# Priority for attention's small VectorE operations, and a scan carry of four operations, in a two-layer hybrid decoder trunk

## The chip, the cores and the metric

The kernel runs on one core of one Trainium2 chip. The metric is the device time of one execution in microseconds (us). Before the change it is 2682.31 us, the median of three runs (2680.16 to 2685.91).

## The reference, cut to what matters

The reference is a trunk of two layers on a residual stream of 256 tokens by 2048 features, all in float32. In each layer one input projection makes queries, keys and values (8 heads), the input of a state-space branch (1024 wide) and two gates.

- Branch A is a causal differential attention. Each head has two score maps; both go through a softmax, and the second map, times a learned lambda, is subtracted from the first. The weighted values are divided by their root mean square per head (`lax.rsqrt(mean(o^2) + 1e-5)`) and scaled.
- Branch B is a diagonal complex state-space model: 64 groups of 16 channels, each driving 64 complex states, scanned causally over the 256 tokens: `h[t] = a * h[t-1] + B u[t]`, `y = Re(C h) + D u`, then GELU and a gated linear unit.

Each branch has its own up-projection; the two are gated, summed and go through an output projection. Layer norm, an MLP with squared ReLU (2048 to 8192 to 2048) and a second layer norm follow.

## The kernel before, in words

**The matmuls.** Every float32 weight and activation is split into a high part, rounded to the type float32r, and a low part, the rest. A product is three matmuls: high by high, high by low, low by high. Weights come in chunks of 512 KB through one DMA queue (line 337). For each chunk ScalarE writes the high part `whi` (line 142) and VectorE the low part `wlo` (line 144); there are three buffers of each, and one chunk is prepared ahead (`AHEAD = 1`). The matmuls of a chunk are at lines 469, 470 and 473 (`tok_mul`, tokens on the output's rows), 544 to 546 (`gemm_feat`) and 567 (`gemm_up`); the one at line 470 reads `wlo`.

**The background.** Attention (`attn_gen`) and the state-space branch (`ssm_gen`) are Python generators. After each weight chunk of the projections the program takes some of their steps (`bg.pump`), so their instructions are traced in between the chunks'. They fill VectorE and ScalarE while TensorE multiplies. `bg.finish(agen)` traces what is left of attention before the attention up-projection, which reads attention's result `ahl`, and `bg.finish(sgen)` what is left of the scan before the gated linear unit.

**The order on each engine** is fixed when the program is built. A planner (Tile's scheduler, with a timeline of its own, `schedule_with_timeline_sim=True`) gives each engine, whenever the engine is free on that timeline, the instruction with the lowest priority number among those that it takes to be ready. The number is the place in the traced order. Inside `with tc.high_priority():` an instruction counts as from the program's start, and so goes ahead of everything that is ready with it. The kernel already does this in two places: the three operations of the rotary embedding (lines 927 to 929) and the gate of the attention up-projection (line 1001).

**Attention's chain, for each pair of heads** (four pairs in a layer). For each head: scores on TensorE (line 789), maxima on VectorE (796), exponentials with their sums on ScalarE (799), the sums' reciprocals (802) and the second one times minus lambda (803) on VectorE, the second map scaled on ScalarE (805), the two maps combined on VectorE (806), transposes on TensorE (811). For the pair: the product with the values (817 to 819), squares with their sums on ScalarE (823), the mean (825) and the inverse root on VectorE: a seed (319) and three Newton steps of three operations each (325, 326, 327), every one on the result of the one before; then the scaling on ScalarE (830), transposes on TensorE (835), and the result's high part on ScalarE (838) and low part on VectorE (839).

**The scan** goes over 4 groups in a layer and in each over 4 chunks of 64 tokens, real and imaginary part apart. At each of the 3 boundaries between chunks six small operations on 128x8 elements carry the state on: two copies of the last state (749), two products with the decay `s_r` (731) and two additions to the first input of the next chunk (732). Then two scan instructions follow (735), then the turning of the chunk by complex factors (739 to 745).

Of the kernel before, what the change touches and what calls it, by code (L numbers as in the profile page):

```python
# [11 lines left out]
F32 = mybir.dt.float32  # L12
# [4 lines left out]
ALU = mybir.AluOpType  # L17
# [3 lines left out]
P = 128  # L21
# [9 lines left out]
L = 64  # L31
# [3 lines left out]
RMS_EPS = 1e-5  # L35
# [69 lines left out]
def trunk(ctx: ExitStack, tc: tile.TileContext, A, out):  # L105
    nc = tc.nc
    V, SC, GP, PE = nc.vector, nc.scalar, nc.gpsimd, nc.tensor
# [89 lines left out]
    s_r = const([P, 64], "s_r")  # L197
# [4 lines left out]
    neglam = const([P, DEPTH], "neglam")  # L202
# [118 lines left out]
    def rsqrt(o, v, n):  # L321
        rsqrt_seed(o, v)
        for _ in range(3):
            a = sm([P, n], tag="rsa", bufs=2)
            V.tensor_tensor(a, o, o, op=ALU.mult)
            V.scalar_tensor_tensor(a, a, -0.5, v, op0=ALU.mult, op1=ALU.mult)
            V.scalar_tensor_tensor(o, a, 1.5, o, op0=ALU.add, op1=ALU.mult)
# [328 lines left out]
    def ssm_gen(l, st):  # L656
        lp = l * 32
        e_re = slot([P, 4, 8, L], name="e_re")
        e_im = slot([P, 4, 8, L], name="e_im")
        w = [slot([P, NCH, 8, L], name="sw") for _ in range(2)]  # L660

        def load_c(g):
            cz = tmp.tile([P, 2, 8, 32], F32, tag="cz", name=nm("cz"), bufs=2)
            hold(GP.dma_start(cz, cmem[l][g] if l in cmem else A["cT"][l, g]))
            return cz

        for g in range(4):
            if l in emem:
                for t, e in zip((e_re, e_im), emem[l]):
                    drip.append((t[:, g], e[:, g]))  # L670
            else:
                for step in e_steps(l, g, e_im[:, g], e_re[:, g]):
                    yield 0.1 if isinstance(step, tuple) else step
        cz_next = load_c(0)
        while st["u"] is None:
            yield 0.5

        def operands(i):
            if i == 16:
                return None  # L680
            g, j = i // 4, i % 4
            bs = tmp.tile([P, 2, 2, P], F32, tag="bs", name=nm("bs"), bufs=1)
            us = tmp.tile([P, 2, 256], F32, tag="us", name=nm("us"), bufs=1)
            b = bsplit[l][g // 2][j, :, :, g % 2].rearrange("r m h c -> m r (h c)")
            u = st["split"][g // 2][j, :, :, 2 * (g % 2):2 * (g % 2) + 2].rearrange("r m h t -> (r m) (h t)")
            for m in range(2):
                ms = slice(64 * m, 64 * m + 64)
                GP.dma_start(bs[ms].rearrange("p h c s -> p (h c s)"), b[m][:, None].broadcast_to([32, 2, 512]))
                GP.dma_start(us[ms].rearrange("p h t -> p (h t)"), u)
            return bs, us  # L690

        nxt = operands(0)
        uT = st["u"]
        for g in range(4):
            jj = slice(lp + 8 * g, lp + 8 * g + 8)
            cz = cz_next
            cz_next = load_c(g + 1) if g < 3 else None
            rt = t_bg([P, 8, L])
            SC.activation(rt, s_r[:, jj, None].broadcast_to([P, 8, L]), AF.Copy)
            GP.memset(rt[:, :, 0:1], 0.0)  # L700
            yield 0.1
            if l not in cmem:
                c_steps(l, g, cz)
                yield 2.0
            for k in range(4):
                bs, us = nxt
                bu = psa.tile([P, 2, 2, NCH, L], F32, tag="bu", name=nm("bu"), bufs=1)
                for q in range(2):
                    for ri in range(2):
                        PE.matmul(bu[:, q, ri].rearrange("p a b -> p (a b)"), bs[:, q, ri, :].bitcast(F32R), us[:, q, :].bitcast(F32R), start=True, stop=True)  # L710
                nxt = operands(4 * g + k + 1)
                yield 0.3
                er = e_re[:, g, k::4, None, :].broadcast_to([P, 2, NCH, L])
                ei = e_im[:, g, k::4, None, :].broadcast_to([P, 2, NCH, L])
                wr, wi = (w[ri][:, :, k::4, :].rearrange("p c q t -> p q c t") for ri in range(2))
                ta, tb = t_bg([P, 2, NCH, L]), t_bg([P, 2, NCH, L])
                V.tensor_tensor(wr, bu[:, :, 0], er, op=ALU.mult)
                V.tensor_tensor(ta, bu[:, :, 1], ei, op=ALU.mult)
                V.tensor_tensor(wi, bu[:, :, 1], er, op=ALU.mult)
                yield 1.8  # L720
                V.tensor_tensor(tb, bu[:, :, 0], ei, op=ALU.mult)
                V.tensor_tensor(wr, wr, ta, op=ALU.add)
                V.tensor_tensor(wi, wi, tb, op=ALU.subtract)
                yield 1.8
            rg = rt.rearrange("p a b -> p (a b)")
            er, ei = e_re[:, g], e_im[:, g]
            carry = None
            for c in range(NCH):
                if c > 0:
                    for ri in range(2):  # L730
                        V.tensor_tensor(carry[:, ri, :], carry[:, ri, :], s_r[:, lp + 8 * g:lp + 8 * g + 8], op=ALU.mult)
                        V.tensor_tensor(w[ri][:, c, :, 0], w[ri][:, c, :, 0], carry[:, ri, :], op=ALU.add)
                for ri in range(2):
                    wv = w[ri][:, c].rearrange("p a b -> p (a b)")
                    V.tensor_tensor_scan(wv, rg, wv, 0.0, ALU.mult, ALU.add)
                yield 2.4
                s = [w[0][:, c], w[1][:, c]]
                ta, tb, td = t_bg([P, 8, L]), t_bg([P, 8, L]), t_bg([P, 8, L])
                V.tensor_tensor(ta, s[1], ei, op=ALU.mult)
                V.tensor_tensor(tb, s[0], ei, op=ALU.mult)  # L740
                V.tensor_tensor(td, s[0], er, op=ALU.mult)
                yield 1.8
                V.tensor_tensor(s[1], s[1], er, op=ALU.mult)
                V.tensor_tensor(s[0], td, ta, op=ALU.subtract)
                V.tensor_tensor(s[1], s[1], tb, op=ALU.add)
                if c < NCH - 1:
                    carry = sm([P, 2, 8], tag="carry", bufs=2)
                    for ri in range(2):
                        V.tensor_copy(carry[:, ri, :], s[ri][:, :, L - 1])
                yield 1.8  # L750
            yps = psa.tile([P, 2, 2, 256], F32, tag="bu", name=nm("y"), bufs=1)[:, 0]
            mm = [Chain() for _ in range(4)]
            for h in range(2):
                for ri in range(2):
                    for j in range(4):
                        mm[j](PE.matmul(yps[32 * j:32 * j + 32, h, :], cz[:, ri, 4 * h + j, :], w[ri][:, :, 4 * h + j, :],
                                        start=ri == 0, stop=ri == 1, tile_position=(0, 32 * j)))
            yield 0.3
            y, a = t_bg([P, 2, 256]), t_bg([P, 2, 256])
            uc = uT[:, 2 * g:2 * g + 2, :]  # L760
            for k in range(2):
                SC.activation(y[:, k, :], uc[:, k, :], AF.Copy, scale=dsk[:, l, 2 * g + k:2 * g + k + 1])
            V.tensor_tensor(y, yps, y, op=ALU.add)
            SC.activation(a, y, AF.Square, scale=math.sqrt(GELU_C))
            yield 0.7
            V.scalar_tensor_tensor(a, a, 1.0, y, op0=ALU.add, op1=ALU.mult)
            SC.activation(a, a, AF.Tanh, scale=GELU_K)
            yield 0.7
            V.scalar_tensor_tensor(uc, a, 1.0, y, op0=ALU.add, op1=ALU.mult)
            yield 0.6  # L770

    def attn_gen(l, qT, kT, v, st):
# [3 lines left out]
        for hp in range(4):  # L776
            wT = tmp.tile([P, 3, 2, P], F32, tag="wT", name=nm("wT"), bufs=1)
            for i in range(2):
# [15 lines left out]
                for c in range(2):  # L794
# [4 lines left out]
                        SC.activation(p[c][:, blk, :], scores[c][:, blk, :], AF.Exp, bias=m[:, c, q:q + 1],  # L799
                                      accum_out=s[:, c, q:q + 1])  # L800
                    yield 0.1
                V.reciprocal(s, s)
                V.tensor_scalar(s[:, 1, :], s[:, 1, :], neglam[:, l:l + 1], None, op0=ALU.mult)
                for q, blk in blocks:
                    SC.activation(p[1][:, blk, :], p[1][:, blk, :], AF.Copy, scale=s[:, 1, q:q + 1])
                    V.scalar_tensor_tensor(p[0][:, blk, :], p[0][:, blk, :], s[:, 0, q:q + 1], p[1][:, blk, :],
# [15 lines left out]
            for i in range(4):  # L822
                SC.activation(sq[:, i, :], po[:, i, :], AF.Square, accum_out=ss[:, i:i + 1])
            yield 0.1
            V.tensor_scalar(ss, ss, 1.0 / P, RMS_EPS, op0=ALU.mult, op1=ALU.add)
            rs = sm([P, 4], tag="rs", bufs=2)
            rsqrt(rs, ss, 4)
            an = t_fg([P, 4, P])
            for i in range(4):
                SC.activation(an[:, i, :], po[:, i, :], AF.Copy, scale=rs[:, i:i + 1])  # L830
# [2 lines left out]
            for qt in range(2):  # L833
                for i in range(2):
# [1 line left out]
            o = st["attn"][hp // 2]  # L836
            hh = 2 * (hp % 2)
            SC.activation(o[:, hh:hh + 2, 0, :], pt, AF.Copy, scale=gsub[:, l:l + 1])
            V.scalar_tensor_tensor(o[:, hh:hh + 2, 1, :], pt, gsub[:, l:l + 1], o[:, hh:hh + 2, 0, :].bitcast(F32),
                                   op0=ALU.mult, op1=ALU.subtract)  # L840
            yield 0.7

    def ln_consts(l, i):
# [361 lines left out]
```

## Time and profile before

| | |
|---|---|
| median of three runs | 2682.31 us (2680.16 to 2685.91) |
| the profiled execution's own time | 2682.85 us |
| its span, first to last instruction | 2681.1 us |
| TensorE (PE) busy | 2642.8 us, 99% |
| VectorE (DVE) busy | 1909.8 us, 71% |
| ScalarE (ACT) busy | 1308.3 us, 49% |
| GpSimd (POOL) busy | 139.4 us, 5% |
| mean granted TensorE clock | 0.996 |

The lines of a profile name an engine (PE matmul, PEld weight load, DVE, ACT, POOL), the line of the kernel, the operation and, as `out<-in`, the tiles that it writes and reads. A line of a timeline begins with the start and the duration in us, and `x2` at its end joins two such instructions in a row. What stands in brackets is the engine's idle time ahead of the instruction and what ended it. Matmuls are pipelined, so that one that is shown as 0.39 us long starts the next after 0.23 us; TensorE's pace is read from the starts.

### The profile page before, as it was taken

The numbers are of one execution on the slowest core, as the hardware profiler recorded it, in microseconds if no ns is written. First come the engines' busy times: TensorE is split into PE (matmuls) and PEld (weight loads), VectorE is DVE, ScalarE is ACT, GpSimd is POOL, SyncE is SP. The second block draws the span as 40 slices with busy tenths as digits, with TensorE's granted clock in tenths as the row PEclk, the third lists the DMA queues.
The fourth block names the chain that finished last, engine by engine and source line by source line (L and its number), as shares of the span: only waits on it lengthen the run. The fifth ranks groups of instructions, "written<-read, shape, count | busy, mean of one in ns | idle before, by whom it ended". The sixth has DMA issues, their size and how long they took to land. (4 is left out here: it accounts for less than half of the span.)

```text
span 2681.1 us, 37176 instructions
## 1 busy us (share of the span) xinstructions
PE 2642.8 (99%) x14144; PEld 2250.5 (84%) x14144; DVE 1909.8 (71%) x2685; ACT 1308.3 (49%) x1756; POOL 139.4 (5%) x289
## 2 busy tenths in 40 slices
PE   8999999999999999999999999999999999999998
PEld 8988878888888888888899878778888888888886
DVE  7899899666765576655659899878676655556556
ACT  5565554444554454543445555544445534435442
POOL 1101100000000000000011100001010000000000
PEclk9999999999999999999999999999999999999999
DMA  8756655674655676666577556557746665555673
GB/s 300 221 169 195 200 181 181 208 247 130 209 189 189 221 229 208 213 200 200 204 232 227 190 177 195 178 161 239 247 143 196 189 196 189 189 196 188 190 245 130
DMA packets 148947, 535.69 MB, mean 200 GB/s; under 512 B 18688, under 2 KB 18976, under 8 KB 147744
## 3 DMA queue, kind: packets, MB, share of 16 engines
q1 hardware_dynamic: 133488, 482.40, 55.7%
q0 software_dynamic: 15280, 50.91, 6.2%
q8 instruction: 111, 1.82, 0.3%
q14 instruction: 68, 0.56, 0.1%
HBM read 517.52 MB, written 15.73 MB: 199 GB/s over the span
## 5 line engine op out<-in xcount | busy, mean ns | idle before, releaser
L144 DVE TENSOR_TENSOR wlo<-w,whi 128x1024 fp32r<-128x1024 f32 (+1 forms) x884 | 1077.2, 1220 | 610.7 <-ACT whi L142 610.2
L142 ACT ACTIVATE whi<-w 128x1024 fp32r<-128x1024 f32 (+1 forms) x884 | 934.6, 1058 | 1035.6 <-PE g L473 649.0
L567 PE MATMUL g<-xT,whi 128*128 128x512 f32 x1920 | 654.4, 395 | 0.0
L567 PE MATMUL g<-xT,wlo 128*128 128x256 f32 x1920 | 496.9, 279 | 0.0
L567 PEld LDWEIGHTS g<-xT,whi 128*128 128x128 f32 x1920 | 344.4, 188 | 64.1
L567 PEld LDWEIGHTS g<-xT,wlo 128*128 128x128 f32 x1920 | 361.5, 188 | 20.8 <-DVE wlo L144 0.3
L470 PE MATMUL g<-wlo,hT 128*128 128x512 f32 x972 | 378.2, 389 | 0.0
L469 PE MATMUL g<-whi,hT 128*128 128x512 f32 x972 | 378.2, 389 | 0.0
L473 PE MATMUL g<-whi,hT 128*128 128x512 f32 x972 | 299.1, 389 | 0.0
L470 PE MATMUL g<-wlo,xT 128*128 128x512 f32 x680 | 268.3, 395 | 1.5 <-DVE wlo L144 1.5
L469 PE MATMUL g<-whi,xT 128*128 128x512 f32 x680 | 267.0, 395 | 1.3 <-ACT whi L142 1.3
L544 PE MATMUL g<-xT,whi 128*128 128x256 f32 x768 | 216.7, 286 | 5.8 <-ACT whi L142 5.8
L545 PE MATMUL g<-xT,whi 128*128 128x256 f32 x768 | 216.7, 285 | 0.0
L469 PEld LDWEIGHTS g<-whi,hT 128*128 128x128 f32 x972 | 182.5, 188 | 38.0
L470 PEld LDWEIGHTS g<-wlo,hT 128*128 128x128 f32 x972 | 182.4, 188 | 37.9
L473 PEld LDWEIGHTS g<-whi,hT 128*128 128x128 f32 x972 | 182.4, 188 | 37.8
L546 PE MATMUL g<-xT,wlo 128*128 128x256 f32 x768 | 211.2, 286 | 2.3 <-DVE wlo L144 2.3
L473 PE MATMUL g<-whi,xT 128*128 128x512 f32 x680 | 212.3, 392 | 0.0
L544 PEld LDWEIGHTS g<-xT,whi 128*128 128x128 f32 x768 | 149.0, 194 | 6.1 <-ACT whi L142 6.0
L470 PEld LDWEIGHTS g<-wlo,xT 128*128 128x128 f32 x680 | 128.2, 189 | 28.2 <-DVE wlo L144 2.6
L469 PEld LDWEIGHTS g<-whi,xT 128*128 128x128 f32 x680 | 128.4, 189 | 27.0 <-ACT whi L142 2.1
L473 PEld LDWEIGHTS g<-whi,xT 128*128 128x128 f32 x680 | 127.4, 188 | 27.1 <-issue 0.4
(292 smaller groups left out, 3196.6 us busy)
## 6 DMA issues: line engine op xcount, KB each, us to landing
w<-in_w_in_dram SPq DMA_DIRECT2D x253, 512.0 KB, 3.8
w<-in_w_mlp_down_dram SPq DMA_DIRECT2D x243, 512.0 KB, 3.5
w<-in_w_mlp_up_dram SPq DMA_DIRECT2D x240, 512.0 KB, 3.6
w<-in_w_out_dram SPq DMA_DIRECT2D x54, 512.0 KB, 4.2
w<-in_w_attn_up_dram SPq DMA_DIRECT2D x32, 512.0 KB, 3.6
w<-in_w_ssm_up_dram SPq DMA_DIRECT2D x32, 512.0 KB, 3.7
us<-usplit POOLq DMA_DIRECT2D x64, 128.0 KB, 4.9
bs<-bsplit POOLq DMA_DIRECT2D x64, 128.0 KB, 4.7
```

What stands on the lines that cost most here:

```text
L142: SC.activation(hi, src, AF.Copy, scale=scale)
L144: V.tensor_tensor(lo, src, hi.bitcast(F32), op=ALU.subtract)
L469: mm(PE.matmul(ps[tt], act(kt)[:, 0, ts], hi[:, k, :], start=kt == 0, stop=False))
L470: mm(PE.matmul(ps[tt], act(kt)[:, 0, ts], lo[:, k, :], start=False, stop=False))
L473: mm(PE.matmul(ps[tt], act(kt)[:, 1, ts], hi[:, k, :], start=False, stop=kt == nkt - 1))
L544: m(PE.matmul(o, wh, ah, start=first and b % 2 == 0, stop=False))
L545: m(PE.matmul(o, wh, al, start=False, stop=False))
L546: m(PE.matmul(o, wl, ah, start=False, stop=last and b % 2 == 1))
L567: mm[j](PE.matmul(o, wt, mv, start=kt == 0 and i == 0, stop=last and i == 1))
```

## The change

The product with the decay moves from ahead of the addition to where the state was copied, and takes the copy's place: the carry is written as the last state times `s_r`, so that two of six operations at each boundary go. And four spots of attention come to stand under `tc.high_priority()`: the softmax sums (802, 803), the mean and the inverse root (825, 319 to 327), and the low part (839).

```diff
             for c in range(NCH):
                 if c > 0:
                     for ri in range(2):
-                        V.tensor_tensor(carry[:, ri, :], carry[:, ri, :], s_r[:, lp + 8 * g:lp + 8 * g + 8], op=ALU.mult)
                         V.tensor_tensor(w[ri][:, c, :, 0], w[ri][:, c, :, 0], carry[:, ri, :], op=ALU.add)
...
                     for ri in range(2):
-                        V.tensor_copy(carry[:, ri, :], s[ri][:, :, L - 1])
+                        V.tensor_tensor(carry[:, ri, :], s[ri][:, :, L - 1], s_r[:, lp + 8 * g:lp + 8 * g + 8], op=ALU.mult)
...
-                V.reciprocal(s, s)
-                V.tensor_scalar(s[:, 1, :], s[:, 1, :], neglam[:, l:l + 1], None, op0=ALU.mult)
+                with tc.high_priority():
+                    V.reciprocal(s, s)
+                    V.tensor_scalar(s[:, 1, :], s[:, 1, :], neglam[:, l:l + 1], None, op0=ALU.mult)
...
-            V.tensor_scalar(ss, ss, 1.0 / P, RMS_EPS, op0=ALU.mult, op1=ALU.add)
             rs = sm([P, 4], tag="rs", bufs=2)
-            rsqrt(rs, ss, 4)
+            with tc.high_priority():
+                V.tensor_scalar(ss, ss, 1.0 / P, RMS_EPS, op0=ALU.mult, op1=ALU.add)
+                rsqrt(rs, ss, 4)
...
-            V.scalar_tensor_tensor(o[:, hh:hh + 2, 1, :], pt, gsub[:, l:l + 1], o[:, hh:hh + 2, 0, :].bitcast(F32),
-                                   op0=ALU.mult, op1=ALU.subtract)
+            with tc.high_priority():
+                V.scalar_tensor_tensor(o[:, hh:hh + 2, 1, :], pt, gsub[:, l:l + 1], o[:, hh:hh + 2, 0, :].bitcast(F32),
+                                       op0=ALU.mult, op1=ALU.subtract)
```

## Rows read from the trace of the kernel before

**Rows 1.** The page's first part: busy us, share of the span, instructions.

```profile
PE 2642.8 (99%) x14144; PEld 2250.5 (84%) x14144; DVE 1909.8 (71%) x2685; ACT 1308.3 (49%) x1756; POOL 139.4 (5%) x289
```

**Rows 2.** The stretch where layer 1's attention ends: busy times, granted clock.

```profile
core 0: us, PE busy (x) PEld busy (x) DVE busy (x) ACT busy (x) POOL busy (x), PEclk, DMA share, GB/s
...
1750.00:1800.00 50.00, 45.09 (x213) 34.87 (x212) 39.47 (x67) 19.45 (x24) 0.00 (x0) 0.93 0.52 157
```

**Rows 3.** Waits of PE, 1744 to 1772 us: total us, times, longest us.

```profile
PE g L470 <- DVE wlo L144: 1.8, 3, 0.9
...
PE g L469 <- ACT ahl L838: 1.7, 1, 1.7
...
PE aux L835 <- ACT at L830: 1.4, 1, 1.4
```

**Rows 4.** Timeline of PE, 1761 to 1772 us.

```profile
1761.25 0.39 PE L470 MATMUL g<-wlo,ahl 128*128 128x512 f32 x1
1761.47 0.61 PE L473 MATMUL g<-whi,ahl 128*128 128x512 f32 x2
1763.49 1.10 PE L835 MATMUL aux<-ident,at 128*128 128x128 f32 x4 [1.40 <-ACT at L830]
1766.28 0.80 PE L469 MATMUL g<-whi,ahl 128*128 128x512 f32 x1 [1.69 <-ACT ahl L838]
1766.88 0.63 PE L470 MATMUL g<-wlo,ahl 128*128 128x512 f32 x1
...
1771.57 0.49 PE L469 MATMUL g<-whi,ahl 128*128 128x512 f32 x1
```

**Rows 5.** Timeline of DVE, 1749 to 1763 us: first and last of the inverse root.

```profile
1749.09 0.16 DVE L825 TENSOR_SCALAR ss<-ss 128x4 f32<-128x4 f32 x1
...
1750.45 0.16 DVE L319 TENSOR_SCALAR rs<-ss 128x4 int32<-128x4 int32 x1
...
1754.36 0.13 DVE L327 SCALAR_TENSOR_TENSOR rs<-rsa,rs 128x4 f32<-128x4 f32 x1
...
1762.26 0.15 DVE L327 SCALAR_TENSOR_TENSOR rs<-rsa,rs 128x4 f32<-128x4 f32 x1
```

**Rows 6.** Timeline of ACT around it: the last sum of squares, the scaling.

```profile
1746.46 0.22 ACT L823 ACTIVATION_READ_ACCUMULATOR at<-aux 128x1 f32 x1
...
1763.09 1.13 ACT L830 ACTIVATE at<-aux,rs 128x128 f32<-128x128 f32 x4
```

**Rows 7.** Timeline of DVE: softmax sums of layer 1's last head.

```profile
1727.90 0.17 DVE L802 RECIPROCAL sx<-sx 128x4 f32<-128x4 f32 x1
...
1731.35 0.20 DVE L803 TENSOR_SCALAR sx<-sx,neglam 128x2 f32<-128x2 f32 x1
```

**Rows 8.** Timeline of DVE, 1515 to 1519 us: two operations that have priority already.

```profile
1515.06 0.68 DVE L928 TENSOR_TENSOR at<-at,rope_s 128x512 f32<-128x512 f32 x1
...
1518.59 0.68 DVE L929 TENSOR_TENSOR kT<-kT,at 128x512 f32<-128x512 f32 x1
```

**Rows 9.** Timeline of PE, 424 us: layer 0, where its attention ends.

```profile
424.64 0.50 PE L470 MATMUL g<-wlo,ahl 128*128 128x512 f32 x1 [1.71 <-DVE wlo L144]
```

**Rows 10.** Tile carry: count and duration ns min/median/max.

```profile
L731 DVE TENSOR_TENSOR carry<-carry,s_r x48: 134/157/168, 147.4 to 1762.0; 128x8 f32<-128x8 f32 x48
```

**Rows 11.** Timeline of DVE, 427 us: one boundary between chunks.

```profile
427.11 0.24 DVE L731 TENSOR_TENSOR carry<-carry,s_r 128x8 f32<-128x8 f32 x2
427.32 0.25 DVE L732 TENSOR_TENSOR sw<-sw,carry 128x8 f32<-128x8 f32 x2
```

**Rows 12.** Timelines: layer 1's last turned chunk; ScalarE behind the product that reads it.

```profile
1769.37 0.68 DVE L745 TENSOR_TENSOR sw<-sw,ss 128x512 f32<-128x512 f32 x1
...
1809.22 0.60 ACT L1016 ACTIVATE at<-g 128x512 f32<-128x512 f32 x1 [1.22 <-PE g L546]
```

**Rows 13.** Groups of DVE by line: the low part.

```profile
L839 DVE SCALAR_TENSOR_TENSOR ahl<-aux,gsub,ahl 128x512 fp32r<-128x512 f32 x8 | 5.9, 738 | 0.0
```

**Rows 14.** Line 825: what its engine sat idle for ahead of it (us, times).

```profile
  ACT at L823: 2.0, 2
```

## The prediction
> **What bounds the kernel now.** I read the page's busy times first. PE is busy 2642.8 of 2681.1 us and no other engine over 71% [rows 1], so only what makes PE wait, or slows its clock, is worth anything; VectorE's own time is not. Then I read the busy times and the granted clock in stretches of 50 us. Outside the start and the end most stretches show PE full and the clock at 1.00; the worst is 1750 to 1800 us, where PE has 45.1 of 50 us and the clock is 0.93 [rows 2]. It is where layer 1's attention ends and the up-projection reads its last part. Then the waits of that stretch: the first transposes wait for the scaling of line 830, the next matmul for attention's high part of line 838, and three matmuls for a low part of the weights [rows 3].
>
> PE's timeline prices it. The pair of matmuls that starts at 1761.47 would let the next start at about 1761.93 (two at 0.23). The next weight matmul starts at 1766.28, 4.35 us later; about 0.45 of that is the four transposes' own work (my estimate: 128 columns each against 512, with room for their start), so 3.9 us are lost. Behind it the pace is wrong too: from 1766.88 to 1771.57 there are eleven starts, 0.43 us each in place of 0.23, and the one at 1766.28 takes 0.60, in all 2.2 + 0.4 = 2.6 us [rows 4]. [...] **The stall costs 3.9 + 2.6 = 6.5 us.** The three waits for low weights come on top with 1.8 us in the view of waits [rows 3].
>
> Why is line 830 late? The sums of squares end on ScalarE at 1746.68, and the scaling that needs their inverse root starts at 1763.09 [rows 6]. In between VectorE runs eleven operations, each on the result of the one before, from 1749.09 to 1762.41 [rows 5]. They are 0.15 us each, 1.7 us in all; the other 11.6 us are ten gaps in which VectorE did low parts and scan work that the planner put first or that was ready while the chain was not.
>
> **The change part by part.**
>
> *Priority for the inverse root (825, 319 to 327).* For the stall to go, 830 must start about 4.4 us earlier. The start can gain up to 2.4 us (1746.68 to 1749.09), less what is then running on VectorE; I take 1.6. The ten gaps mean 1.16 us [rows 5]. If priority leaves one foreign operation in a gap, mostly one of 0.7 [rows 8, 12] and at times a low part or a small one, a gap is about 0.8 and the chain 3.5 us shorter. Bounds: 9.9 us (every gap falls to the 0.17 of one small operation) and nothing, for the kernel has such a link already: line 929 hangs on 928, both have priority, and it starts 3.53 us later, 2.85 of them a gap [rows 8]. I take 3.5, for the chain's gaps are mostly shorter than that one, and a small operation leaves the engine sooner.
>
> *Priority for the softmax sums (802, 803).* In layer 1's last head 803 starts 3.45 us after 802, on which it hangs [rows 7]; with one foreign operation between it would be 0.8 to 1.4. Gain to the head's chain 2 us, bounds 0 and 3.3. Together 1.6 + 3.5 + 2 = 7.1 us, over the 4.4 that are needed. What is then late next is PE itself, which has the weights' matmuls to do.
>
> *Priority for the low part (839).* Eight of 0.74 us [rows 13], each needed some matmuls after the high part. In layer 1 it no longer holds anything once 838 is early; I take 0.
>
> *The moved operations push others back.* Now 16 x (0.17 + 0.20) + 8 x 1.7 + 5.9 = 25 us of VectorE work, the same as before, go ahead of low weights and scan [rows 5, 7, 13]. A low weight behind one is late by 0.15 to 0.74 us, and PE waits only where it has no slack: three such waits in the last stretch [rows 3] and one of 1.71 us in layer 0 [rows 9], whose inverse root stands in the same disorder. The sign is open: the chain out of the way could free those 1.8 + 1.7 = 3.5 us, or new waits like them could come in their place. Bounds -3.5 and +3.5, I take -0.5, since the scans that delay them stay. On ScalarE the scalings of 805 and 830 move forward with their inputs, ahead of a high weight or two. No DMA is issued by a moved step, and SP's and POOL's queues keep their order; no wait is added that has no counterpart before.
>
> *The carry.* 48 products go [rows 10]; the copies become products of the same shape, 0.16 us, at no cost. A pair takes 0.21 us of VectorE's time, from its start to the next pair's [rows 11], so 24 boundaries give 5.0 us (upper bound 48 x 0.157 = 7.5) and one link less in the scan's chain. [...] To PE it is worth nothing in layer 1: the last turned chunk ends at 1770.05, and the product that reads it ends at 1809.22 [rows 12]; if that cover were gone, at most half of the 5.0 us would be on PE's path. In layer 0 the scan ends nearer to its use; I take 0 there, bounds -1 and 0.
>
> **Sum:** -6.5 (stall and clock) - 0.5 (low weights) + 0 + 0 = -7.0 us against the profiled execution's 2682.85. That lies 0.5 us over the median of the runs; from the median of 2682.31 I get **2675.3 us**.
>
> **The rivals.**
>
> *Part of it (the chain is shorter, but not by 4.4 us).* For it speaks the link of 3.53 us between operations that have priority [rows 8]. With 2 us gained, 1.9 us of waits and half of the slow clock stay: -2.0 - 1.3 = -3.3, about 2679.
>
> *The change does not do what it says.* If the gaps come from the planner's own idea of when a result is there, priority changes nothing: the chain's operations already slip in whenever they are ready. The link between 928 and 929, with priority and yet as long as two of the chain's [rows 5, 8], fits that; the 3.45 us ahead of 803 [rows 7] speak against it. Then only the carry is left, about 2682, within what can be told apart.
>
> *Slower: the head of VectorE's queue blocks.* An operation that is put forward may stand in VectorE's order before ScalarE has made its input; then all low weights behind it wait. 32 moved operations are fed by ScalarE or by PE and ScalarE (16 of 802, 8 of 825, 8 of 839). Before the change two of the eight 825s left the engine idle, 1.0 us each [rows 14]. Priced at 1.0 us where PE has no slack, seven places eat the 6.5 us, and 12 make it slower by 5.5; 14 give 2689. Against it: VectorE is busy 39 of 50 us where it matters most [rows 2], so most idle microseconds are absorbed. [...]
>
> **How the numbers follow.** A measurement of this kernel can tell about 0.2%, 5.4 us, from no change: faster means under 2676.9, slower over 2687.7. The forecast gets 0.55: its stall goes, its time is 2675.3, its own range 2668 to 2679 by the bounds of the low weights and the clock. Part of it gets 0.14, no effect 0.19, the blocked queue 0.12. Of the forecast 0.48 lies under 2676.9, of the part 0.03; all of the blocked queue but 0.01 is over 2687.7. So faster 0.51, slower 0.11, same 0.38. The range takes in the forecast down to 2668 and the two middle cases with 3 us for moved low weights, 2668 to 2685; the blocked queue and some of the forecast's far end are left out.
>
> **What would show it.** Right: after the last squares of layer 1 the eleven operations take under 10 us, PE has no wait for 830 or 838 there, the stretch's clock is back at 1.00, line 731 counts no longer, and 749 is a product, 48 times. Part: a wait for 838 of 1 to 2 us and a clock below 1.00. Wrong: the gaps in the chain unchanged, or new idle time of VectorE ahead of 802, 825 or 839 with PE waiting for a low weight behind it. The forecast would also be wrong if the planner, with other orders on ScalarE, made a new wait in a stretch that is full now, for a wait of some 2 us costs its slow clock as well [rows 4].

## The result and the profile after

The changed kernel takes 2699.69 us, the median of six runs (2695.72 to 2703.64), against 2682.48 us for the kernel before on the same chip (2680.16 to 2685.91, six runs): a ratio of 1.0063, 95% interval 1.0054 to 1.0073. It is slower by 17 us, where 7 us less were forecast. The range, 2668 to 2685, does not hold it.

The profiled execution after took 2700.26 us with a span of 2698.5 us. The first line of its page, which answers to [rows 1]:

```profile
PE 2647.8 (98%) x14144; PEld 2252.2 (83%) x14144; DVE 1907.3 (71%) x2637; ACT 1308.3 (48%) x1756; POOL 139.3 (5%) x289
```

VectorE has its 48 operations less. PE has as many matmuls as before. Its span grew by 17.4 us, its busy time by 5.0; so it stands idle for 50.7 us in place of 38.3, 12.4 more, and the rest of the loss is a slower pace: the mean granted clock is 0.993 in place of 0.996. The next view tells where: the busy times by stretch, for the two stretches in which a layer's attention ends (columns: PE, PEld, DVE, ACT, POOL busy with their instructions, granted TensorE clock, DMA share, GB/s). The kernel after:

```profile
400.00:450.00 50.00, 40.87 (x183) 32.93 (x184) 48.82 (x85) 22.37 (x40) 2.08 (x4) 0.94 0.51 158
1750.00:1800.00 50.00, 40.14 (x189) 29.92 (x188) 43.63 (x77) 19.31 (x33) 0.00 (x0) 0.90 0.41 127
```

The kernel before, the stretch in layer 0 (the one in layer 1 is [rows 2]):

```profile
400.00:450.00 50.00, 48.29 (x226) 39.88 (x226) 47.58 (x79) 21.54 (x33) 2.07 (x4) 1.00 0.61 181
```

PE lost 7.4 us of busy time in layer 0 and 5.0 in layer 1, and 7.4 + 5.0 is the whole 12.4; elsewhere small gains and losses cancel. The clock fell from 1.00 to 0.94 in layer 0. The step from 0.93 to 0.90 in layer 1 is too small to read: with the priority alone (below) the waits of before come with 0.97 in one execution. PE's waits after, in layer 0's stretch, then in layer 1's (total us, times, longest):

```profile
PE aux L836 <- ACT at L831: 6.8, 1, 6.8
PE g L470 <- DVE wlo L144: 1.6, 1, 1.6
PE g L469 <- ACT ahl L839: 0.8, 1, 0.8
...
PE aux L836 <- ACT at L831: 6.5, 1, 6.5
PE g L470 <- DVE wlo L144: 2.5, 2, 1.3
PE g L469 <- ACT ahl L839: 0.9, 1, 0.9
```

Line 836 is 835 of before, 831 is 830. So this is the wait of [rows 3], of 1.4 us there: the last pair's transposes wait for the scaling, which waits for the inverse root. It is 6.5 us now, and layer 0, which had none, has one of 6.8 us. Around the latter PE's timeline shows:

```profile
437.90 0.61 PE L473 MATMUL g<-whi,ahl 128*128 128x512 f32 x2
445.31 1.25 PE L836 MATMUL aux<-ident,at 128*128 128x128 f32 x4 [6.80 <-ACT at L831]
447.34 0.80 PE L469 MATMUL g<-whi,ahl 128*128 128x512 f32 x1 [0.78 <-ACT ahl L839]
447.93 0.63 PE L470 MATMUL g<-wlo,ahl 128*128 128x512 f32 x1
```

The next matmul behind the waiting transposes reads what they lead to, and waits in its turn. No matmul came ahead of the waiting one here, but these lines do not show whether one whose inputs are there could, since the next matmul depends on the transposes. The run with five operations, further down, has such a pair:

```profile
405.34 1.20 PE L710 MATMUL bu<-us,bs 128*128 128x256 f32 x4 [2.49 <-DMA us<-usplit]
406.33 0.63 PE L470 MATMUL g<-wlo,xT 128*128 128x512 f32 x1
```

The matmul of line 470 had its low weights by 404.09 us at the latest, the end of VectorE's last low part before it, and yet started only behind the one of line 710 that waited for a DMA. Here a matmul whose inputs were there waited behind one whose were not.

What did priority do to the chain? VectorE's timeline, layer 1's last pair, after (line 827 is 825 of before):

```profile
1765.19 0.16 DVE L827 TENSOR_SCALAR ss<-ss 128x4 f32<-128x4 f32 x1
1765.27 0.68 DVE L743 TENSOR_TENSOR sw<-ss,ss 128x512 f32<-128x512 f32 x1
1765.87 1.22 DVE L144 TENSOR_TENSOR wlo<-w,whi 128x1024 fp32r<-128x1024 f32 x1
1767.01 0.68 DVE L744 TENSOR_TENSOR sw<-sw,ss 128x512 f32<-128x512 f32 x1
1767.61 0.16 DVE L319 TENSOR_SCALAR rs<-ss 128x4 int32<-128x4 int32 x1
...
1780.38 0.14 DVE L327 SCALAR_TENSOR_TENSOR rs<-rsa,rs 128x4 f32<-128x4 f32 x1
```

Three foreign operations still stand between the first two links, and from the first link's start to the last's it is 15.2 us, where it was 13.2 [rows 5]. So two things have to be told apart: whether the priority or the carry made attention late, and why.

### The profile page after: what moved, and what is told of

It reads as the page before. It is cut to its first block, busy times and chain, and to the rows that moved or that the text cites. A ratio compares the mean times of both kernels' runs of the same rounds, so it can differ in the third digit from the quotient of the medians.

```text
span 2698.5 us, 37121 instructions
## 1 busy us (share of the span) xinstructions
PE 2647.8 (98%) x14144; PEld 2252.2 (83%) x14144; DVE 1907.3 (71%) x2637; ACT 1308.3 (48%) x1756; POOL 139.3 (5%) x289
```

## The experiments

At first three theories were open. **1:** the shorter carry makes the scan earlier, and attention, which fills the scan's holes, late. **2:** the priority blocks VectorE's queue. **3:** any small edit throws the planner's order about. After the first four runs they were sharpened into theories A to E of the later expectations.

This table gathers all runs: the median, the ratio to the kernel before as run beside it on the same chip, PE's busy time in the two stretches of 50 us (400 to 450, 1750 to 1800), and, counted in the order of TensorE's instructions, how many matmuls on low weights stand ahead of the last pair's last transposes in layers 0 and 1 (the place). At 728 and 3200 the transposes stand last of all that can be done without them.

| kernel | us | ratio (95%) | PE 400 to 450 | PE 1750 to 1800 | place |
|---|---|---|---|---|---|
| before | 2682.48 | | 48.29 | 45.09 | 720, 3200 |
| after | 2699.69 | 1.0063 (1.0054 to 1.0073) | 40.87 | 40.14 | 728, 3200 |
| carry alone | 2698.25 | 1.0059 (1.0045 to 1.0073) | 41.72 | 40.14 | 728, 3200 |
| priority alone | 2682.15 | 0.9998 (0.9989 to 1.0007) | 48.20 | 45.07 | 720, 3200 |
| product and copy | 2683.11 | 0.9998 (0.9989 to 1.0007) | 48.28 | 45.45 | 720, 3200 |
| eight operations | 2694.09 | 1.0038 (1.0026 to 1.0051) | 44.61 | 40.34 | 728, 3200 |
| carry, TensorE first | 2679.07 | 0.9985 (0.9976 to 0.9994) | 50.00 | 45.39 | 708, 3200 |
| carry, swapped | 2686.14 | 1.0012 (1.0003 to 1.0021) | 49.51 | 43.78 | 696, 3200 |
| swap only | 2690.55 | 1.0024 (1.0014 to 1.0034) | 49.70 | 44.72 | 700, 3200 |
| five operations | 2683.44 | 1.0003 (0.9994 to 1.0012) | 45.77 | 46.88 | 720, 3196 |
| before, TensorE first | 2677.04 | 0.9980 (0.9971 to 0.9989) | 49.70 | 47.89 | 704, 3196 |
| after, TensorE first | 2680.04 | 0.9993 (0.9984 to 1.0002) | 49.99 | 45.41 | 708, 3200 |
| layer 1, slower background | 2704.80 | 1.0089 (1.0074 to 1.0104) | 50.00 | 47.02 | 708, 3192 |
| five, swapped | 2682.23 | 0.9997 (0.9988 to 1.0006) | 50.00 | 46.94 | 700, 3196 |

In layer 1 the last place says little: it is 3200 with 45.09 us busy and with 40.14. One step up the chain, the transposes of the last head (line 811) tell more. In the traces they stand behind 3172 such matmuls before, with the priority alone and with product and copy; behind 3180 after and with the carry alone, 3184 with eight operations, 3176 with the swapped carry, and 3168 or 3169 in all the others. From 3176 on the stretch is emptier than before: attention is late there already ahead of its last steps.

**The carry alone.** The edit is the first two hunks of the change, and the attention part as before:

```diff
-                        V.tensor_tensor(carry[:, ri, :], carry[:, ri, :], s_r[:, lp + 8 * g:lp + 8 * g + 8], op=ALU.mult)
...
-                        V.tensor_copy(carry[:, ri, :], s[ri][:, :, L - 1])
+                        V.tensor_tensor(carry[:, ri, :], s[ri][:, :, L - 1], s_r[:, lp + 8 * g:lp + 8 * g + 8], op=ALU.mult)
```

> The carry of four operations alone, no new priority. Theory 1 (the shorter carry lets the planner serve the scan earlier, attention then finds fewer holes on VectorE, comes late and PE waits at its end in both layers): 2695 to 2703 us, the time of the whole change, with attention's low parts of layer 0 later by 10 us or more and the waits of PE at the end of attention about as long as after the change. Theory 2 (the priority blocks VectorE's queue): 2677 to 2683. Theory 3 (any small edit throws the planner's order about, with either sign): any time from 2670 to 2700, not bound to the lateness of attention.

Measured: 1.0059, the loss of the whole change; PE's waits at the ends of attention were 3.9 + 2.5 us in layer 0 and 6.5 + 0.9 in layer 1. Attention's low parts of layer 0 came later by 6.7, 14.0, 3.7 and 9.4 us for the four pairs: late, but two of the four by less than the 10 us expected. The carry does it.

**The priority alone.** The edit is the remaining hunks.

```diff
+                with tc.high_priority():
+                    V.reciprocal(s, s)
+                    V.tensor_scalar(s[:, 1, :], s[:, 1, :], neglam[:, l:l + 1], None, op0=ALU.mult)
...
+            with tc.high_priority():
+                V.tensor_scalar(ss, ss, 1.0 / P, RMS_EPS, op0=ALU.mult, op1=ALU.add)
+                rsqrt(rs, ss, 4)
...
+            with tc.high_priority():
+                V.scalar_tensor_tensor(o[:, hh:hh + 2, 1, :], pt, gsub[:, l:l + 1], o[:, hh:hh + 2, 0, :].bitcast(F32),
+                                       op0=ALU.mult, op1=ALU.subtract)
```

> The four spots of priority alone, the carry as before. Theory 1: 2680 to 2685 us, the same as before, for nearly the whole order of the instructions stays as it was and the inverse root's chain takes 13 us as before. Theory 2: 2693 to 2703. The prediction on record would have given some 2676 to 2680 here.

Measured: 0.9998. VectorE's timeline, the softmax sums of layer 1's last head, then the first and the last link of its last pair:

```profile
1727.14 0.17 DVE L803 RECIPROCAL sx<-sx 128x4 f32<-128x4 f32 x1
...
1730.59 0.20 DVE L804 TENSOR_SCALAR sx<-sx,neglam 128x2 f32<-128x2 f32 x1
...
1748.33 0.16 DVE L828 TENSOR_SCALAR ss<-ss 128x4 f32<-128x4 f32 x1
...
1761.49 0.16 DVE L327 SCALAR_TENSOR_TENSOR rs<-rsa,rs 128x4 f32<-128x4 f32 x1
```

The chain takes 13.2 us, as before [rows 5], and from the first of the softmax sums to the second it is 3.45 us, as before [rows 7]. Of the eight pairs' chains none is more than 0.4 us shorter than before. Set side by side, the two orders differ in 20 of VectorE's 2685 instructions. Theory 2 falls, and so does the step of the prediction that the whole gain came from.

**Product and copy: the arithmetic without the missing link.** The decay is multiplied where the copy was, and a copy of the carry onto itself stands where the product was.

```diff
-                        V.tensor_tensor(carry[:, ri, :], carry[:, ri, :], s_r[:, lp + 8 * g:lp + 8 * g + 8], op=ALU.mult)
+                        V.tensor_copy(carry[:, ri, :], carry[:, ri, :])
...
-                        V.tensor_copy(carry[:, ri, :], s[ri][:, :, L - 1])
+                        V.tensor_tensor(carry[:, ri, :], s[ri][:, :, L - 1], s_r[:, lp + 8 * g:lp + 8 * g + 8], op=ALU.mult)
```

> The decay is multiplied where the state was copied, as in the change, but a copy of the carry onto itself takes the place of the removed product: six operations and as many links as before, the order of the instructions the same as before. Theory 1: 2680 to 2685 us; the product instead of the copy costs nothing, only the missing link and the missing operations matter. If the product that reads the strided last state were itself slow: above 2685, with line 748 longer than 0.16 us.

Measured: 0.9998, and the tile's rows (count, duration ns min/median/max) give the product on the strided state a duration like the copy's:

```profile
L749 DVE TENSOR_TENSOR carry<-sw,s_r x48: 150/158/168, 142.9 to 1759.6; 128x8 f32<-128x8 f32 x48
L731 DVE COPY carry<-carry x48: 133/163/174, 145.3 to 1759.8; 128x8 f32<-128x8 f32 x48
```

Every instruction stood in the place of its counterpart. So the new operation costs nothing, and what costs is only that two operations and a link are gone.

**Eight operations: the reverse dose.**

```diff
+                        V.tensor_copy(carry[:, ri, :], carry[:, ri, :])
                         V.tensor_tensor(carry[:, ri, :], carry[:, ri, :], s_r[:, lp + 8 * g:lp + 8 * g + 8], op=ALU.mult)
```

> The reverse dose: two operations more at each boundary (a copy of the carry onto itself ahead of its product), one link more in the scan's chain. Theory 1: the scan comes later and attention earlier; 2672 to 2685 us, no slower than before, with attention's low parts in layer 0 earlier than before. Theory 3: the order is thrown about again, and the time may be as slow as 2690 to 2700 with attention late in one pair or the other.

Measured: 1.0038, and the waits came at the same two places (2.6 + 0.8 us and 7.6 + 0.8 us). Theory 1 as I had put it, with a direction, falls: a longer carry makes attention late as well. The order was dealt anew, as theory 3 has it, and the loss again lay at the ends of attention.

**What makes attention late.** With the carry alone the orders part first on VectorE, at 145 us, where a low part and an addition of the scan change places, then on ScalarE at 163 us and on TensorE at 177 us. What it comes to on TensorE shows in the first head pair of layer 0. The timeline of PE there without the weights' matmuls, first before, then with the carry alone (789 and 788 are the scores, 756 and 755 the scan's products `y`, 710 its inputs; the lines of attention's transposes and of the mask are left out):

```profile
180.89 0.49 PE L789 MATMUL aux<-kT,qT 64*128 64x128 f32 x2
...
181.68 0.70 PE L789 MATMUL aux<-kT,qT 64*128 64x256 f32 x2
...
187.97 0.92 PE L789 MATMUL aux<-kT,qT 64*128 64x128 f32 x4
...
191.79 0.64 PE L756 MATMUL y<-sw,cz 128*32 128x256 f32 x8
```

```profile
177.42 0.48 PE L788 MATMUL aux<-kT,qT 64*128 64x128 f32 x2
...
180.80 0.70 PE L788 MATMUL aux<-kT,qT 64*128 64x256 f32 x2
...
183.25 1.93 PE L755 MATMUL y<-sw,cz 128*32 128x256 f32 x32
...
190.23 0.64 PE L710 MATMUL bu<-us,bs 128*128 128x256 f32 x4
...
192.41 0.92 PE L788 MATMUL aux<-kT,qT 64*128 64x128 f32 x4
```

With the carry alone the head's first scores start 3.5 us earlier than before (177.42 against 180.89), for the scan's group is done sooner and everything has moved up a little. But now the scan's products and inputs, and the weights' matmuls between them, have gone ahead of the second map's scores, which come 4.4 us later than before. Softmax, transposes and values hang on them. That gave theory A.

**TensorE first, with the carry.** All five places where attention uses TensorE get priority, and VectorE's four have none. Two of the places stand here; the mask (792), the products with the values (817 to 819) and the last transposes (835) are wrapped in the same way:

```diff
-                        mm[c](PE.matmul(scores[c][:, ks, :], qT[pr, h, qt * P:qt * P + P], kT[pr, h, 0:P * (qt + 1)],
-                                        start=qt == 0, stop=False, tile_position=(64 * c, 0)))
+                        with tc.high_priority():
+                            mm[c](PE.matmul(scores[c][:, ks, :], qT[pr, h, qt * P:qt * P + P], kT[pr, h, 0:P * (qt + 1)],
+                                            start=qt == 0, stop=False, tile_position=(64 * c, 0)))
...
-                    PE.transpose(pt[:, b, :], p[0][:, b, :], ident)
+                    with tc.high_priority():
+                        PE.transpose(pt[:, b, :], p[0][:, b, :], ident)
```

> The carry of four operations, and priority for attention's operations on TensorE (scores, transposes, products with the values) in place of those on VectorE. Theory A (the shorter carry changes the order so that attention's matmuls stand behind the scan's and the weights' on TensorE, each head comes later, and PE runs dry where the last pair is needed): 2681 to 2689 us, the loss of 12 to 14 us at the end of attention in layer 0 gone, and in layer 1 at most as large as with the carry alone. Theory B (VectorE has too little room for attention once the scan's chain is shorter; TensorE's order does not matter, as priority on VectorE did not): 2694 to 2702, as with the carry alone.

Measured: 0.9985, 19 us less than the carry alone, and 2 us under theory A's 2681 to 2689. The same scores, then the scan's products, on PE:

```profile
177.84 0.92 PE L789 MATMUL aux<-kT,qT 64*128 64x128 f32 x4
...
183.72 0.92 PE L789 MATMUL aux<-kT,qT 64*128 64x128 f32 x4
...
184.57 0.28 PE L793 MATMUL aux<-mask,ident 128*128 128x256 bf16 x1
...
185.48 1.93 PE L755 MATMUL y<-sw,cz 128*32 128x256 f32 x32
```

And the two stretches:

```profile
400.00:450.00 50.00, 50.00 (x225) 41.10 (x224) 49.62 (x79) 23.05 (x28) 0.00 (x0) 1.00 0.56 178
1750.00:1800.00 50.00, 45.39 (x237) 36.27 (x236) 38.04 (x51) 19.45 (x24) 0.00 (x0) 0.97 0.51 162
```

Layer 0 is full, at clock 1.00, though VectorE is as full as after the change (49.6 of 50 us). The inverse root of layer 0's last pair starts 18.7 us earlier than with the carry alone and is itself only 2.4 us shorter (first and last link, first with the carry alone, then here):

```profile
418.39 0.14 DVE L824 TENSOR_SCALAR ss<-ss 128x4 f32<-128x4 f32 x1
...
435.83 0.15 DVE L327 SCALAR_TENSOR_TENSOR rs<-rsa,rs 128x4 f32<-128x4 f32 x1
```

```profile
399.69 0.17 DVE L830 TENSOR_SCALAR ss<-ss 128x4 f32<-128x4 f32 x1 [0.90 <-ACT at L828]
...
414.69 0.16 DVE L327 SCALAR_TENSOR_TENSOR rs<-rsa,rs 128x4 f32<-128x4 f32 x1
```

So nearly all of the gain lies ahead of VectorE's chain. B falls, and A holds for layer 0: the loss there goes with the turn that attention gets on TensorE. That it is the scan's products, rather than the weights' matmuls between them, that hold the scores up was not taken apart. Nor does this run alone exclude that the edit merely dealt a luckier order; the same priority on two other kernels, below, bears on that. In layer 1 the stretch is no fuller than before the change, for PE still waits for both halves of attention's result (844 and 845 are 838 and 839 of before):

```profile
PE g L473 <- DVE ahl L845: 1.9, 1, 1.9
PE g L469 <- ACT ahl L844: 1.3, 1, 1.3
```

**The carry, swapped.** The carry alone, with two neighbours of the scan's input stage exchanged; neither reads the other's result.

```diff
-                V.tensor_tensor(ta, bu[:, :, 1], ei, op=ALU.mult)
                 V.tensor_tensor(wi, bu[:, :, 1], er, op=ALU.mult)
+                V.tensor_tensor(ta, bu[:, :, 1], ei, op=ALU.mult)
```

> The carry of four operations, and in the scan's input stage two neighbouring products that do not depend on each other (ta, wi) change places: the same work, the same links. In this order attention's last pair of layer 0 is served some 32 matmuls on low weights earlier than with the carry alone. Theory C (it is the particular order that costs, any small edit deals a new one): 2681 to 2690 us, layer 0's loss gone. Theory D (a shorter chain of the scan pushes attention back as such): 2692 to 2702.

Measured: 1.0012, 12 us less than the carry alone, from an exchange that takes no work away. Layer 0's waits for attention are gone; in layer 1 they are 2.5 + 0.8 us. The short carry itself therefore does not push attention back (D); the order that came with it did (C).

**The swap only,** on the kernel before, the same exchange.

> The kernel before with nothing but those two products exchanged. Theory C: layer 0 has little left to lose less of, layer 1 keeps its stall, so 2678 to 2685 us although some 740 of TensorE's instructions and 490 of VectorE's have changed places. If any disturbance of the order costs because the kernel stood on a lucky one: 2688 to 2700.

Measured: 1.0024, some 7 us slower: a miss of C's number. The ends of attention are about as before (busy 49.70 and 44.72 us). PE's waits over the whole span show small ones elsewhere:

```profile
PE g L470 <- DVE wlo L144: 8.2, 11, 1.7
...
PE bu L710 <- DMA us<-usplit: 4.9, 2, 3.1
...
PE bu L710 <- DMA bs<-bsplit: 1.8, 1, 1.8
```

In the kernel before these are 5.8 us (7 times), 2.8 us (twice) and none. The place of the last pair is thus not the whole of an order's price: some 6 us of small waits came with this one.

**Five operations.** The two products become one over both halves; the chain keeps its links.

```diff
+                    V.tensor_tensor(carry, carry, s_r[:, None, lp + 8 * g:lp + 8 * g + 8].broadcast_to([P, 2, 8]), op=ALU.mult)
                     for ri in range(2):
-                        V.tensor_tensor(carry[:, ri, :], carry[:, ri, :], s_r[:, lp + 8 * g:lp + 8 * g + 8], op=ALU.mult)
```

> Five operations at each boundary: the two products with the decay become one over both halves, the chain keeps its three links (copy, product, addition). Theory C: in this order layer 1's last pair is served a little earlier (VectorE's last step of it stands two low weights further ahead) and layer 0 as before: 2674 to 2683 us. Theory D, by the number of operations: between before and the carry of four, 2687 to 2692.

Measured: 1.0003. The waits for attention in layer 1, 3.1 us before, are gone (busy 46.88 us), but others grew over the whole span: for low weights at line 470 to 8.5 us (before 5.8), for the scan's input from DMA to 3.8 us (before 2.8). The longest of the latter is new in layer 0's stretch, which is down to 45.77 us:

```profile
PE bu L710 <- DMA us<-usplit: 2.5, 1, 2.5
```

Theory D's 2687 to 2692, worked out by the number of operations, is not met. Nor is a gain: 2683.44 lies just above theory C's 2674 to 2683, and layer 0 was not as before.

**Before, TensorE first:** the edit of the fifth run, on the kernel before.

> The kernel before, carry of six operations, with priority for attention's operations on TensorE alone. Theory A (what counts is when attention's matmuls get their turn on TensorE; the carry's two operations are worth next to nothing by themselves): 2675 to 2683 us, about the time of the carry of four with the same priority (2679). If the carry of four does bring something once the order is right: 2 to 5 us above that one.

Measured: 0.9980, interval 0.9971 to 0.9989, the fastest of all and clearly below the kernel before. Its stretch in layer 1:

```profile
1750.00:1800.00 50.00, 47.89 (x265) 38.94 (x266) 40.83 (x60) 21.16 (x27) 0.00 (x0) 1.00 0.56 179
```

No wait for the scaling or the high part is left there, and the clock is at 1.00: the stall that the prediction wanted to remove is gone, by another edit. The whole gain is 4.3 us (2681.34 us of the kernel before beside it). The carry of four brings nothing on top; its ratio with the same priority is 0.9985.

**After, TensorE first:** the same edit on the whole change.

> The whole change with priority for attention's operations on TensorE on top. Theory A: 2676 to 2684 us, some 18 us less than the change, the four spots of priority on VectorE being worth nothing here either. If those spots block VectorE's queue once attention comes early: above 2685.

Measured: 0.9993 (0.9984 to 1.0002), by the ratios 19 us less than the change, and not to be told from the kernel before. The four spots on VectorE are worth nothing here either: in layer 1 PE waits 2.0 us for attention's low part, although line 839 is one of the spots. Three kernels with this priority, and this background in layer 1, thus lie at or below the kernel before (0.9985, 0.9980, 0.9993), while none of the six orders without any priority does so beyond its interval. That speaks for the turn on TensorE and against a lucky order, but three are few.

**Layer 1 with a slower background.** On top of the fifth run:

```diff
-RATE = (2.0, 1.8)
+RATE = (2.0, 1.4)
```

> The carry of four, TensorE's priority for attention, and in layer 1 less background per chunk (1.4 in place of 1.8), so that the scan's steps are put in later and attention's last pair ends some two chunks earlier; the scan's last group then ends later, close to the gated linear unit that reads it. Theory E (attention and scan share a full VectorE in this stretch, and one is earlier only at the other's cost): the wait at the end of attention in layer 1 goes, 5 to 8 us, and a wait of 2 to 8 us at the gated linear unit comes in its place; 2674 to 2684. If VectorE has room there: 2668 to 2674.

Measured: 1.0089. The last pair's inverse root in layer 1 ended at 1748.5 in place of 1756.3 us, and the waits for attention's results there are gone. But PE's waits from 1750 to 1860 us, and the next stretch, show the price:

```profile
PE y L755 <- DVE sw L743: 9.9, 1, 9.9
PE g L544 <- ACT ghl L142: 4.7, 1, 4.7
```

```profile
1800.00:1850.00 50.00, 33.52 (x204) 29.02 (x204) 34.68 (x51) 16.38 (x22) 1.35 (x3) 0.78 0.28 94
```

The scan's last products came late, and the gated linear unit with them: 16.5 us of idle time in one stretch and a clock of 0.78 in place of full ones. Theory E named the place of the new wait, with far too small a price (2 to 8 us). Its reason, a full VectorE, is not what the traces show. Ahead of the waits, first in the fifth run, then here, VectorE has 31.66 us of work in place of 45.96:

```profile
1700.00:1750.00 50.00, 49.23 (x230) 39.83 (x229) 45.96 (x80) 25.98 (x47) 2.61 (x6) 1.00 0.58 177
1700.00:1750.00 50.00, 50.00 (x244) 37.29 (x243) 31.66 (x54) 27.34 (x54) 0.11 (x1) 1.00 0.51 167
```

The scan's steps were put in late; attention did not crowd them out. The scan's slack of some 40 us in layer 1 [rows 12] was used up by an edit of one constant.

**Five, swapped:** both small edits at once.

> Five operations at each boundary (one product over both halves) together with the exchange of the two neighbouring products, no priority on TensorE. In this order attention's last pair stands early in layer 0 (as with the exchange alone, 20 matmuls on low weights ahead of the kernel before) and, in layer 1, one chunk's matmuls earlier than before. If the places of the last pairs told the whole of it: 2674 to 2680 us. If an order's cost is also made of small waits elsewhere that these two places do not tell (the exchange alone cost 7 us with a good place in layer 0): 2682 to 2692.

Measured: 0.9997. Both places are good, and the two stretches hold 50.00 and 46.94 us; the gain of 1.7 + 1.9 us there was given back in small waits, as with the swap alone (for low weights at line 470 8.9 us in 9 waits, before 5.8 in 7; new is one of 2.4 us ahead of a line 710). The median of 2682.23 us falls to the second of the two numbers, if by little: the places of the last pairs do not tell the whole.

## Why the prediction was wrong, point by point

**The bound was right, its price is open.** PE is what counts, the end of attention is where it waits, and behind the waits there the clock is lower: in the kernel before it was 0.50 from 1766.28 to 1771.57 us, where the starts are 0.43 us apart [rows 4], and 1.00 from 1772 to 1790; after the change it was 0.50 from 445.30 to 449.50 us, behind the wait of 6.8 us. The change moved the time there, only the other way: 12.4 us more idle time in the two stretches, and over the run 5.0 us more busy time for the same matmuls, with the clock of the stretches at 0.94 and 0.90. The prediction puts that cost on a wait of some 2 us, but not every such wait has it: behind one of 2.59 us ahead of line 710 the clock of the kernel before was 0.53 (112.71 to 116 us), behind the one of 1.71 us in layer 0 [rows 9] the stretch of before stays at 1.00, and so does the stretch in layer 1 with waits of 2.0 and 1.3 us in the whole change with TensorE first. The 6.5 us for the stall in layer 1 are neither confirmed nor refuted. Their 2.6 us of slow clock are one execution's: with the priority alone the same waits come with a clock of 0.97 in place of 0.93. And where the stall went, with TensorE's priority on the kernel before, the 4.3 us are a sum over the whole run, with small waits elsewhere in it (ahead of line 544 they are 8.2 us in place of 6.9, for instance).

**"A gap is about 0.8 and the chain 3.5 us shorter" failed.** With the priority alone the chain takes 13.2 us as before, and the order hardly differs; the 2 us counted for the softmax sums did not come either. The lower bound of that step, nothing, taken from the link of 3.53 us between two operations that already had priority [rows 8], was the true value. I put it aside because the chain's gaps are mostly shorter; the row that was nearest in kind should have been taken, not the hope between two bounds. With it fell the -6.5 of the sum: the stall did not go, and after the change its two waits were 6.5 + 0.9 us in place of 1.4 + 1.7. The nothing taken for the low part (839), "no longer holds anything once 838 is early", did not hold either: with TensorE's priority and the carry of four PE waited for it 1.9 us, and 2.0 us with priority for 839 as well. The rival that the change does not do what it says describes this part, and its price for the priority alone (no difference) was right. Why the planner fills the gaps all the same is not shown: its own timeline is in no trace.

**"To PE it is worth nothing", of the carry, with "bounds -1 and 0" in layer 0, is the step that made the sign wrong.** It priced the operations that go, and they are indeed worth nothing: with the right order, four or six operations give 0.9985 and 0.9980. It gave no bound above zero for what a shorter chain does to a planned order, although the prediction's own last sentence named such a way to be wrong, by other orders on ScalarE. That had no chance and no price; with the carry alone it was 16 us. Of the six edits that changed the order without any priority four were slower than before, by 3 to 16 us (four operations, eight, the swap, four with the swap), and two the same (five, five with the swap); a new order deserved a rival of its own.

**"The head of VectorE's queue blocks" fell.** It had the right sign, 2689, for a wrong reason: the priority alone costs nothing, and after the change PE's long waits are for a late chain, not for low weights behind a blocked operation. An operation behind one that waits can stand still, as in the kernel before: line 326, whose input line 325 had written by 1628.77 us, started at 1630.70, behind line 717, ahead of which VectorE stood idle 0.71 us for PE.

**TensorE's own order was left out.** The prediction went through the queues that the moved steps pass (VectorE, ScalarE, SP, POOL) and took TensorE's as given. By the runs it was the deciding one in layer 0: no hunk of the change names it, and it is busy 99% of the span, nearly all of it with weights' matmuls. There a priority number moved the start of layer 0's last inverse root by 18.7 us; on VectorE, with the carry as before, it moved next to nothing. Why the shorter carry, and the longer one too, led the planner to put attention later stays open.

## What to carry to other kernels

Where a planner lays out the order, an edit's price has two parts: the operations it takes away, and the new order of everything behind them. The second can be the larger one, of either sign, and a run of the edit with the old order kept (here the product plus a copy) separates the two. Before giving priority to a late chain, see on which engine its operations stand behind a backlog of ready work: here that was TensorE, where priority for attention's few small matmuls was worth 19 us with the short carry and 4.3 without it, while priority on VectorE, where the chain's links wait for each other, was worth nothing.

## What was not expected of the hardware

The traces show nothing of the chip that the kernel before had not shown: long stalls with a lower clock behind them, 1.40 and 1.69 us of waits [rows 4] and then a clock of 0.50 in the kernel before, 6.8 and 0.8 us and then 0.50 after the change. What surprised is how little it takes: exchanging two operations that do not depend on each other moved the time by 0.24% one way (kernel before) and by 0.45% the other (short carry, 2698.25 to 2686.14 us), more than the 0.2% over which six runs of the kernel before spread (2680.16 to 2685.91 us).
